# The block of the SSD's time steps as a third lane beside the first two input blocks

## The chip, the cores and the metric

The kernel runs on one core of one Trainium2 chip. The time is device microseconds (us) for one execution of the whole program. Execution times are compared as the median of runs of the same kernel.

## The reference, cut to what matters

One decoder layer over 256 positions and 2048 channels, in float32: a Mamba-2 SSD mixer, a cross-attention into 256 memory tokens, and a gated ConvFFN, each between two RMSNorms. The change lies at the very start, in the norm ahead of the SSD and in the first columns of its input projection:

```python
h = _rmsnorm(x, norm_pre[i, 0])
proj = h @ w_in                       # 2048 x (4096 + 6144 + 64)
z, xbc, dt = jnp.split(proj, ...)     # dt: the last 64 columns, one per head
xbc = silu(_causal_dwconv(xbc, conv_w, conv_b))
xs, bm, cm = jnp.split(xbc, ...)      # 4096, 8*128, 8*128
dt = softplus(dt + dt_bias)
a = dt * (-exp(a_log))
a_cs = cumsum(a, over the 128 positions of a chunk)
decay = exp(a_cs[l] - a_cs[s]) for s <= l
y_diag = (cm @ bm.T * decay) @ (xs * dt)
```

Every y of the SSD needs the decays, and so the time steps dt.

## The kernel before

**Products in three passes.** All large products are done with operands split into a high part in the fp32r type and the rest: `hi` is a copy made by ScalarE, `lo = x - hi` is made by VectorE. TensorE then adds three products, hi·hi, hi·lo and lo·hi (`mm3`, L245 to L248). The split holds for the weights (tiles `raw`, `hi`, `lo`) and for the activations (`H`, high part in columns 0 to 255, low part behind it).

**Blocks and slots.** The weights of a block of 128 output columns are one chunk of 128 x 2048 floats (1 MB): 16 steps k of 128 input channels. A chunk is loaded into one of 3 `raw` buffers on SyncE's queue and split in two halves of 1024 columns; there are 5 `hi` and 5 `lo` buffers. The work is written as a list of slots (`order`, `pos`). A slot holds one or more lanes; a lane is one block with its weights, the moving operand (`movH`), and a function `post` that takes the result out of PSUM. The lanes of a slot run step by step beside each other. Small work hangs on a slot as hooks: at a count of lane steps (`"pe"`), ahead (`early`) or behind (`late`, `tail`). The posts of a slot are written at the start of the next.

The order at the start is: slot 0 with the two lanes C0 and B0, slot 1 with the time steps' block alone (`dt`), then x0, z0, x1, z1, x2, z2, x3, z3, C1, B1 and so on, one block a slot.

**What the program order means.** The tile framework orders the instructions of each engine by a simulated timeline; what comes first in the program has the higher priority, and `hot` (`tc.high_priority`) raises it. `behind(x)` (`tc.issue_after`) keeps an instruction behind another one. On the chip each engine then runs its list in that order.

**The start.** x, transposed, comes in five pieces (`m`) between eight pieces of the two first chunks (512 columns each, `w_first` splits them). `x_h(j)` makes the high and low parts of two channel blocks, scaled by the norm's gain. The norm's factor over the channels is applied later, to the results: `x_sq(j)` squares a pair of channel blocks (ScalarE), `x_norm.add` sums them (VectorE), `pe1` sums over partitions on TensorE, GpSimd takes the power -1/2, `pe2` spreads the result over the partitions, and `rx` is its copy. Every post of the SSD's blocks begins with `x_scaled`, the product with `rx`, and so waits for it.

**The time steps' block.** Its weights are 16 steps of 64 columns (512 KB). High and low part of a step lie side by side as one operand of 128 columns, so that two matmuls a step do (`dt_mm`, L393 and L394), 32 in all; tile `hi` holds steps 0 to 7, tile `lo` steps 8 to 15. Its post leads to the chain `dt2` (softplus on VectorE and ScalarE), `dt3` (cumulative sums on TensorE), `dt4` (transpose, then a transfer to memory), `load_rows` (spread back over the partitions), `decay` (six Relu activations for each pair of heads, L505 to L507) and `decay_exp` (one Exp over four pairs, L512).

**Buffers in PSUM.** Four of the name `pj` take the blocks' results in turn, `pt` and `py` one each, `ms` two.

The names in the profile: L266 and L268 are `hilo` (in the start: the first weights), L270 and L272 are `hilo` with a scale (in the start: the parts of x), L365 the squares, L294 the sums of squares, L304 and L324 the two steps of the norm on TensorE, L332 the copy `rx`, L138 and L152 the split of the time steps' weights, L143 and L157 the splits of all later chunks, L371 `x_scaled`, L462 the Silu of the convolution.

Of the kernel before, what the change touches and what calls it, by code (L numbers as in the profile page):

```python
# [7 lines left out]
F32 = mybir.dt.float32  # L8
FR = mybir.dt.float32r
# [52 lines left out]
def hybrid_layer_kernel(ctx, tc, xT, memT, pvd, alog, w_dt, w_in, w_kv, w_q, w_out, w_o, w_up, w_dn, out):  # L62
# [64 lines left out]
        return G[:, q:q + 2].rearrange("p k n -> p (k n)")  # L127

    def split_hi(c, h):
        kind = chunks[c][2]  # L130
        if kind == "dt":
            if h == 0:
                hi = splitp.tile([128, 1024], FR, name="hi")
                lo = splitp.tile([128, 1024], FR, name="lo")
                hi_t[c, 0], lo_t[c, 0] = hi, lo
                r = raw_t[c][:, :1024].rearrange("p (k n) -> p k n", n=64)
                for t, q in ((hi, 0), (lo, 8)):
                    S.activation(t.rearrange("p (k a n) -> p k a n", a=2, n=64)[:, :, 0], r[:, q:q + 8], AF.Copy)  # L138
            return
        a, b = span(c, h)  # L140
        hi_t[c, h] = g_part(c, h, 0) if c in in_g else splitp.tile([128, 1024], FR, name="hi")
        with behind(B.get("hold_s") if c in held else None):
            S.activation(hi_t[c, h][:, :b - a], raw_t[c][:, a:b], AF.Copy)  # L143

    def split_lo(c, h):
        kind = chunks[c][2]
        if kind == "dt":
            if h == 0:
                r = raw_t[c][:, :1024].rearrange("p (k n) -> p k n", n=64)
                for t, q in ((hi_t[c, 0], 0), (lo_t[c, 0], 8)):  # L150
                    t4 = t.rearrange("p (k a n) -> p k a n", a=2, n=64)
                    V.tensor_tensor(t4[:, :, 1], r[:, q:q + 8], t4[:, :, 0].bitcast(F32), op=OP.subtract)  # L152
            return
        a, b = span(c, h)
        lo_t[c, h] = g_part(c, h, 1) if c in in_g else splitp.tile([128, 1024], FR, name="lo")
        with behind(B.get("hold_v") if c in held else None):
            V.tensor_tensor(lo_t[c, h][:, :b - a], raw_t[c][:, a:b], hi_t[c, h][:, :b - a].bitcast(F32),  # L157
                            op=OP.subtract)
# [203 lines left out]

    def x_sq(j):
        sq = wA.tile([128, 2, T], F32, name="rows" if j else "xacc", bufs=4 if j else 1)
        S.activation(sq, pair(j), AF.Square)  # L365
        x_norm.add(sq)

    def x_scaled(ps, name="ev"):
# [5 lines left out]
    def x_h(j):  # L374
        def fn():
            for k in range(2 * j, 2 * j + 2):
                now(hilo(halves(H[:, k]), m[:, k], col("pre", k)))
        return fn

    def wide(rbc):  # L380
# [7 lines left out]
    rows_d = dram.tile([NH, T], F32, name="rows_d")  # L388

    def dt_mm(c):  # L390
        def fn(ps, k):
            w = (hi_t if k < 8 else lo_t)[c, 0][:, (k % 8) * 128:(k % 8 + 1) * 128]
            PE.matmul(ps[:, :T], w, H[:, k, 0:T], start=(k == 0), stop=False)  # L393
            PE.matmul(ps[:, :T], w, H[:, k, T:], start=False, stop=(k == KD - 1))  # L394
        return fn

    def dt_post(ps):
# [225 lines left out]

    pos = {}
    for kind, i in order:
        pos[kind, i] = 0 if kind == "B" and i == 0 else slot()

    def lane(s, src, n, mov, post, wide=False):
        c = new_chunk(src, n)
# [3 lines left out]
    for kind, i in order:  # L633
        s = pos[kind, i]
        if kind in ("C", "B"):
# [1 line left out]
            lane(s, w_in[blk_no], 2048, movH, bc_post(kind + "T", blk))  # L637
            blk_no += 1
            if kind == "B":
                hook(s + 2 if i else s + 3, "pe", cb_mm(i), 2 if i else 14)  # L640
        elif kind == "dt":
            c_dt = new_chunk(w_dt, 1024, "dt")
            slots[s].lanes.append((c_dt, 0, movH, hot(dt_post), dt_mm(c_dt), False))
            hook(s + 1, "pe", hot(dt2), 2)
            hook(s + 2, "pe", hot(dt3), 4)
            hook(s + 2, "pe", hot(dt4), 11)
        elif kind == "x":
            lane(s, w_in[blk_no], 2048, movH, xs_post(i))
            blk_no += 1
            d = 2 if i < 2 else 0  # L650
            if i == 0:
                for q in range(4):
                    hook(s + 2, "early", hot(load_rows(q)))
                    hook(s + 3, "early", decay(q))
                hook(s + 3, "early", decay_exp)
            elif i % 4 == 0:
                for q in range(4):
                    hook(max(4, s - 9 + 2 * q), "early", load_rows(i + q))
                    hook(s - 7 + 2 * q, "late", decay(i + q))
                hook(s - 1, "late", decay_exp)  # L660
            if i < 2:
                hook(s + 2, "pe", xs_tr(i), 4 if i == 0 else 12)
                hook(s + 2, "late", xdt(i))
                hook(s + 3 if i == 0 else s + 2, "late", mk_m(i))
                hook(s + 4 if i == 0 else s + 3, "pe", y_mm(i), 6 if i == 0 else 10)
                hook(s + 4 if i == 0 else s + 3, "late", y_post(i))
            elif i < NP - 1:
                hook(s + 2, "early", mk_m(i))
                hook(s + 2, "pe", xs_tr(i), 4)
                hook(s + 2, "late", xdt(i))  # L670
                hook(s + 3, "pe", y_mm(i), 6)
                hook(s + 3, "late", y_post(i))
            else:
                hook(s + 1, "pe", xs_tr(i), 14)
                hook(s + 1, "late", mk_m(i))
                hook(s + 1, "late", xdt(i))
                hook(s + 2, "pe", y_mm(i), 6)
                hook(s + 2, "pe", y_post(i), 7)
        elif kind == "z":
            lane(s, w_in[blk_no], 2048, movH, z_post(i))  # L680
            blk_no += 1
        else:
            half = 0 if kind == "wo" else 1
            lane(s, w_out[half * KD + i], 2048, movG, wout_post(half, i), wide=True)
# [358 lines left out]

    for c in (0, 1, 2):
        raw_t[c] = rawp.tile([128, 2048], F32, name="raw")
    for h in range(2):
        for c in (0, 1):
            hi_t[c, h] = splitp.tile([128, 1024], FR, name="hi")  # L1050
# [2 lines left out]
    for j in range(4):  # L1053
# [1 line left out]
            nc.sync.dma_start(raw_t[c][:, 512 * j:512 * (j + 1)], chunks[c][0][:, 512 * j:512 * (j + 1)])  # L1055
        e = min(4 * j + 6, KD)
        nc.sync.dma_start(m[:, 4 * j + 2:e], xT[:, 4 * j + 2:e])
    nc.sync.dma_start(raw_t[2][:, :1024], chunks[2][0])
    nc.sync.dma_start(pv[:, PV["cw"]:], pvd[:, PV["cw"]:])
    nc.sync.dma_start(nega, bass.AP(tensor=alog.tensor, offset=alog.offset, ap=[[0, 128], [1, NH]]))  # L1060
    state.update(dma=3, hi=4, lo=4)
    make_consts()

    ps = psum.tile([128, 512], F32, name="ms", bufs=2)
# [3 lines left out]
    def w_first(j):  # L1068
        for c in (0, 1):
            q = slice(512 * (j % 2), 512 * (j % 2) + 512)  # L1070
            now(hilo((hi_t[c, j // 2][:, q], lo_t[c, j // 2][:, q]), raw_t[c][:, 512 * j:512 * (j + 1)]))

    for j in range(KD // 2):
        if j % 2 == 0:
            hook(0, "pe", lambda j=j: w_first(j // 2), 4 * j)
        hook(0, "pe", x_h(j), 4 * j)
        hook(0, "tail", lambda j=j: x_sq(j))
    hook(0, "tail", x_norm.split)
    hook(0, "tail", hot(x_norm.pe1))
# [2 lines left out]
    for i, s in enumerate(slots):  # L1082
# [1 line left out]
        need = max(ln[0] for ln in s.lanes) + 1  # L1084
        state["limit"] = 2 * min(ln[0] for ln in s.lanes) + SPLIT_BUFS
        if i == 0:
            state["limit"] = 4
        if first_up - 4 <= i < first_up:
            state["limit"] += PRE[i - first_up + 4]
        if i == first_up:  # L1090
# [15 lines left out]
        lanes = s.lanes  # L1106
        nk = max([len(ln[2]) for ln in lanes], default=0)
        cnt = 0
        names = ("pj", "pj", "pt", "py") if i == first_up else ("pj",) * 4
        pss = [psum.tile([128, 512], F32, name=n, bufs=4 if n == "pj" else 1) if ln[5] is not None else None  # L1110
               for ln, n in zip(lanes, names)]
        hooks = dict(hk.pe)
# [135 lines left out]
```

## Time and profile before

| | |
|---|---|
| median of 3 runs | 1559.93 us (1558.48 to 1560.27) |
| profiled execution | 1559.15 us |
| its span, first to last instruction | 1557.3 us |
| outside the span | 1.85 us |
| TensorE busy | 1541.5 us (99%) |
| VectorE busy | 1199.2 us (77%) |
| ScalarE busy | 963.9 us (62%) |
| granted TensorE clock, mean | 0.997 |

Matmuls are pipelined, and a matmul's busy time overlaps that of the next, so that a busy share of TensorE does not say that it ran at its peak. Times in rows are us from the start of the span, durations of single instructions are in us or ns as said. A timeline merges like instructions that follow each other: x4 and 1.71 us means four of them within 1.71 us.

### The profile page before, as it was taken

How to read it: one execution, taken by the hardware profiler on the slowest of the kernel's cores; microseconds unless marked ns; L12 is line 12 of the kernel's file. 1: busy time of each engine (PE TensorE's matmuls, PEld its weight loads, DVE VectorE, ACT ScalarE, POOL GpSimd, SP SyncE). 2: the span in 40 equal slices, each digit the busy share in tenths (PEclk: the TensorE clock that was granted, in tenths of full speed). 3: DMA queues.
4: the chain of work that ended last, by engine and by line, in shares of the span. 5: the costliest groups of instructions: out<-in, count | busy, mean ns of one | idle time of the engine just before them, and what ended most of it. 6: DMA issues, size and time to landing. Idle time of an engine off the chain costs nothing. (4 is left out here: it accounts for less than half of the span.)

```text
span 1557.3 us, 26009 instructions
## 1 busy us (share of the span) xinstructions
PE 1541.5 (99%) x10364; PEld 1418.0 (91%) x10364; DVE 1199.2 (77%) x1903; ACT 963.9 (62%) x1566; POOL 11.3 (1%) x16
## 2 busy tenths in 40 slices
PE   9999999999999999999989999999999999999998
PEld 8999999989999999889888888888888888888886
DVE  7699989755898987969788878655787866778774
ACT  7698887644777774856566655544555533555553
POOL 0000000000000000000000000000000000000000
PEclk9999999999999999999999999999999999999999
DMA  7665555655455554854444555555555555555452
GB/s 278 212 217 189 174 203 190 194 191 184 162 204 177 167 186 136 324 189 165 161 153 146 194 190 189 192 183 199 190 191 191 184 187 198 194 192 189 151 212 78
DMA packets 50937, 292.10 MB, mean 188 GB/s; under 512 B 5568, under 2 KB 9728, under 8 KB 23936
## 3 DMA queue, kind: packets, MB, share of 16 engines
q1 hardware_dynamic: 50096, 289.34, 54.3%
q8 instruction: 81, 1.33, 0.3%
q10 hardware_dynamic: 720, 1.11, 0.2%
q14 instruction: 40, 0.33, 0.1%
HBM read 288.26 MB, written 2.16 MB: 186 GB/s over the span
## 5 line engine op out<-in xcount | busy, mean ns | idle before, releaser
L143 ACT ACTIVATE hi<-raw 128x1024 fp32r<-128x1024 f32 (+2 forms) x518 | 539.9, 1045 | 480.9 <-PE pj L252 378.4
L157 DVE TENSOR_TENSOR lo<-raw,hi 128x1024 fp32r<-128x1024 f32 (+2 forms) x518 | 624.4, 1207 | 252.7 <-ACT hi L143 247.9
L252 PE MATMUL pj<-H,hi 128*128 128x512 f32 x1344 | 466.6, 392 | 1.1 <-DVE ev L931 1.1
L252 PE MATMUL pj<-G,hi 128*128 128x512 f32 x1202 | 417.1, 392 | 0.0
L246 PE MATMUL pj<-H,hi 128*128 128x256 f32 x1344 | 379.1, 283 | 1.3 <-ACT hi L266 0.8
L248 PE MATMUL pj<-H,lo 128*128 128x256 f32 x1344 | 377.9, 282 | 0.8 <-DVE lo L268 0.7
L247 PE MATMUL pj<-H,hi 128*128 128x256 f32 x1344 | 377.8, 281 | 0.0
L253 PE MATMUL pj<-H,lo 128*128 128x256 f32 x1344 | 376.2, 280 | 0.0
L253 PE MATMUL pj<-G,lo 128*128 128x256 f32 x1202 | 335.8, 280 | 0.0
L252 PEld LDWEIGHTS pj<-H,hi 128*128 128x128 f32 x1344 | 252.3, 188 | 57.0 <-ACT hi L143 1.3
L252 PEld LDWEIGHTS pj<-G,hi 128*128 128x128 f32 x1202 | 225.4, 188 | 49.5
L246 PEld LDWEIGHTS pj<-H,hi 128*128 128x128 f32 x1344 | 253.3, 189 | 3.2 <-ACT hi L266 1.6
L248 PEld LDWEIGHTS pj<-H,lo 128*128 128x128 f32 x1344 | 253.3, 189 | 2.1 <-DVE lo L268 1.7
L247 PEld LDWEIGHTS pj<-H,hi 128*128 128x128 f32 x1344 | 253.7, 189 | 1.2 <-DVE H L272 0.2
L253 PEld LDWEIGHTS pj<-H,lo 128*128 128x128 f32 x1344 | 252.5, 188 | 0.1
L253 PEld LDWEIGHTS pj<-G,lo 128*128 128x128 f32 x1202 | 225.8, 188 | 0.4
L941 DVE SCALAR_TENSOR_TENSOR fu<-ev,pv,fu 128x255 f32<-128x255 f32 (+1 forms) x176 | 84.3, 480 | 2.8
L460 DVE SCALAR_TENSOR_TENSOR u<-ev,pv,u 128x255 f32<-128x255 f32 (+2 forms) x144 | 68.7, 479 | 5.1 <-ACT u L456 3.9
L937 ACT ACTIVATE fu<-ev,pv 128x256 f32<-128x256 f32 x88 | 51.7, 589 | 1.4 <-DVE ev L934 0.9
L371 DVE TENSOR_TENSOR ev<-pj,rx 128x256 f32<-128x256 f32 x80 | 33.7, 422 | 13.4 <-PE pj L248 10.7
L266 ACT ACTIVATE Mh<-dec 128x768 fp32r<-128x768 f32 x32 | 26.9, 841 | 16.4 <-PE py L248 15.6
L934 DVE TENSOR_TENSOR ev<-ev,rb 128x256 f32<-128x256 f32 x84 | 35.5, 422 | 1.4
(287 smaller groups left out, 1461.7 us busy)
## 6 DMA issues: line engine op xcount, KB each, us to landing
raw<-in_w_up_dram SPq DMA_DIRECT2D x88, 1024.0 KB, 4.8
raw<-in_w_in_dram SPq DMA_DIRECT2D x78, 1024.0 KB, 4.9
raw<-in_w_out_dram SPq DMA_DIRECT2D x32, 1024.0 KB, 4.8
raw<-in_w_dn_dram SPq DMA_DIRECT2D x32, 960.0 KB, 4.7
raw<-in_w_dn_dram SPq DMA_DIRECT2D x16, 896.0 KB, 4.4
rows<-rows_d SPq DMA_DIRECT2D x32, 256.0 KB, 4.4
raw<-in_w_kv_dram SPq DMA_DIRECT2D x4, 1024.0 KB, 4.8
raw<-in_w_kv_dram SPq DMA_DIRECT2D x8, 512.0 KB, 4.3
```

The costliest lines, as they stand in the source:

```text
L143: S.activation(hi_t[c, h][:, :b - a], raw_t[c][:, a:b], AF.Copy)
L157: V.tensor_tensor(lo_t[c, h][:, :b - a], raw_t[c][:, a:b], hi_t[c, h][:, :b - a].bitcast(F32), op=OP.subtract)
L246: PE.matmul(ps, whi, xhi, start=start, stop=False)
L247: PE.matmul(ps, whi, xlo, start=False, stop=False)
L248: B["mm"] = PE.matmul(ps, wlo, xhi, start=False, stop=stop)
L252: PE.matmul(ps, whi, x, start=start, stop=False)
L253: B["mm"] = PE.matmul(ps[:, T:], wlo, x[:, 0:T], start=False, stop=stop)
L371: V.tensor_tensor(t, ps[:, :T], x_norm.rbc, op=OP.mult)
L460: V.scalar_tensor_tensor(u[:, d:], ps[:, :T - d], pv[:, w + j:w + j + 1], u[:, d:], op0=OP.mult, op1=OP.add)
L934: V.tensor_tensor(t, t, B["n4"].rbc, op=OP.mult)
L937: S.activation(u, t, AF.Identity, bias=col("fb", blk), scale=pv[:, w + 2:w + 3])
L941: V.scalar_tensor_tensor(u[:, d:], t[:, :T - d], pv[:, w + j:w + j + 1], u[:, d:], op0=OP.mult, op1=OP.add)
```

## The change

The time steps' block moves from slot 1 into slot 0 as a third lane, and all later slots move up by one. In the lane, a step of the time steps runs four steps behind the two others (`max(0, i - 4)`), and the last five run at the end. Its result goes to the PSUM buffer `pt` in place of a `pj`.

Its raw weights land in the tile `dec` (which the decays use later) and no longer in the third `raw` buffer. They come in two halves of 256 KB, behind the pieces 0 and 2 of x, not at the end. The load of the following chunk (x0) is issued at once, into the third `raw` buffer, ahead of the rest of the parameter vectors (`pv`) and of `nega`. The split of the time steps' weights is written between the splits of x (`dt_split`, at j = 1 and 5).

The squares of x are put behind the last high part of x on ScalarE (`behind(B["x_hi"])`).

The hooks of slot 0 move from 4j to 6j, since three lanes count three steps; the hooks `dt2`, `dt3`, `dt4` move from the counts 2, 4, 11 to 8, 8, 14 of the same blocks (x0, z0), and `cb_mm(0)` stays at z0.

```diff
     def x_sq(j):
         sq = wA.tile([128, 2, T], F32, name="rows" if j else "xacc", bufs=4 if j else 1)
-        S.activation(sq, pair(j), AF.Square)
+        with behind(B["x_hi"]):
+            S.activation(sq, pair(j), AF.Square)
         x_norm.add(sq)
...
             for k in range(2 * j, 2 * j + 2):
-                now(hilo(halves(H[:, k]), m[:, k], col("pre", k)))
+                hi, lo = halves(H[:, k])
+                B["x_hi"] = S.activation(hi, m[:, k], AF.Copy, scale=col("pre", k))
+                V.scalar_tensor_tensor(lo, m[:, k], col("pre", k), hi.bitcast(F32), op0=OP.mult, op1=OP.subtract)
...
     def dt_mm(c):
-        def fn(ps, k):
-            w = (hi_t if k < 8 else lo_t)[c, 0][:, (k % 8) * 128:(k % 8 + 1) * 128]
-            PE.matmul(ps[:, :T], w, H[:, k, 0:T], start=(k == 0), stop=False)
-            PE.matmul(ps[:, :T], w, H[:, k, T:], start=False, stop=(k == KD - 1))
+        def fn(ps, i):
+            for k in range(max(0, i - 4), i - 3 if i < KD - 1 else KD):
+                w = (hi_t if k < 8 else lo_t)[c, 0][:, (k % 8) * 128:(k % 8 + 1) * 128]
+                PE.matmul(ps[:, :T], w, H[:, k, 0:T], start=(k == 0), stop=False)
+                PE.matmul(ps[:, :T], w, H[:, k, T:], start=False, stop=(k == KD - 1))
...
-        pos[kind, i] = 0 if kind == "B" and i == 0 else slot()
+        pos[kind, i] = 0 if (kind, i) in (("B", 0), ("dt", 0)) else slot()
...
-                hook(s + 2 if i else s + 3, "pe", cb_mm(i), 2 if i else 14)
+                hook(s + 2, "pe", cb_mm(i), 2 if i else 14)
...
-            hook(s + 1, "pe", hot(dt2), 2)
-            hook(s + 2, "pe", hot(dt3), 4)
-            hook(s + 2, "pe", hot(dt4), 11)
+            hook(s + 1, "pe", hot(dt2), 8)
+            hook(s + 2, "pe", hot(dt3), 8)
+            hook(s + 2, "pe", hot(dt4), 14)
...
-    for c in (0, 1, 2):
+    for c in (0, 1):
         raw_t[c] = rawp.tile([128, 2048], F32, name="raw")
+    raw_t[2] = dec.rearrange("p a n -> p (a n)")
...
         nc.sync.dma_start(m[:, 4 * j + 2:e], xT[:, 4 * j + 2:e])
-    nc.sync.dma_start(raw_t[2][:, :1024], chunks[2][0])
+        if j in (0, 2):
+            nc.sync.dma_start(raw_t[2][:, 256 * j:256 * j + 512], chunks[2][0][:, 256 * j:256 * j + 512])
+    issue_dma(3)
     nc.sync.dma_start(pv[:, PV["cw"]:], pvd[:, PV["cw"]:])
...
-    state.update(dma=3, hi=4, lo=4)
+    state.update(dma=4, hi=6, lo=6)
...
+    def dt_split(j):
+        if j == 0:
+            hi_t[2, 0] = splitp.tile([128, 1024], FR, name="hi")
+            lo_t[2, 0] = splitp.tile([128, 1024], FR, name="lo")
+        t = (hi_t, lo_t)[j][2, 0].rearrange("p (k a n) -> p k a n", a=2, n=64)
+        now(hilo((t[:, :, 0], t[:, :, 1]), raw_t[2][:, 512 * j:512 * j + 512].rearrange("p (k n) -> p k n", n=64)))
...
         if j % 2 == 0:
-            hook(0, "pe", lambda j=j: w_first(j // 2), 4 * j)
-        hook(0, "pe", x_h(j), 4 * j)
+            hook(0, "pe", lambda j=j: w_first(j // 2), 6 * j)
+        hook(0, "pe", x_h(j), 6 * j)
+        if j in (1, 5):
+            hook(0, "pe", lambda j=j: dt_split(j // 4), 6 * j)
         hook(0, "tail", lambda j=j: x_sq(j))
...
         if i == 0:
-            state["limit"] = 4
+            state["limit"] = 6
...
-        names = ("pj", "pj", "pt", "py") if i == first_up else ("pj",) * 4
+        names = ("pj", "pj", "pt", "py") if i in (0, first_up) else ("pj",) * 4
```

Also removed are the branches of `split_hi` and `split_lo` that split the time steps' weights before.

## Rows read from the trace of the kernel before

**Rows 1.** The page, part 1: busy us, share of the span, instructions
```profile
PE 1541.5 (99%) x10364; PEld 1418.0 (91%) x10364; DVE 1199.2 (77%) x1903; ACT 963.9 (62%) x1566; POOL 11.3 (1%) x16
```

**Rows 2.** Windows: length, busy (instructions) of PE, PEld, DVE, ACT, POOL; PEclk, DMA share, GB/s
```profile
6.60:10.00 3.40, 2.91 (x18) 2.51 (x18) 1.69 (x4) 1.42 (x5) 0.00 (x0) 1.00 0.93 310
10.00:15.00 5.00, 4.12 (x30) 3.51 (x30) 4.86 (x11) 5.00 (x11) 0.00 (x0) 1.00 1.04 410
15.00:20.00 5.00, 4.64 (x34) 3.92 (x33) 5.00 (x11) 5.00 (x12) 0.00 (x0) 1.00 0.38 145
...
30.00:40.00 10.00, 10.00 (x87) 10.00 (x87) 9.22 (x16) 8.49 (x14) 0.00 (x0) 1.00 0.86 299
```

**Rows 3.** Timeline of PE, 6 to 29 us: start, us, instruction
```profile
6.66 0.56 PE L246 MATMUL pj<-H,hi 128*128 128x256 f32 x1
...
12.01 0.38 PE L246 MATMUL pj<-H,hi 128*128 128x256 f32 x1 [0.80 <-ACT hi L266]
...
23.55 0.95 PE L304 MATMUL ms<-ones,xacc 128*128 128x1 f32 x8
24.36 0.36 PE L393 MATMUL pj<-H,hi 128*128 128x256 f32 x1
24.56 0.28 PE L394 MATMUL pj<-H,hi 128*128 128x256 f32 x1
...
27.61 0.28 PE L394 MATMUL pj<-H,lo 128*128 128x256 f32 x1
...
28.42 0.28 PE L246 MATMUL pj<-H,hi 128*128 128x256 f32 x1
```

**Rows 4.** Timeline of ACT, 8 to 22 us
```profile
8.68 1.71 ACT L270 ACTIVATE H<-m,pv 128x256 fp32r<-128x256 f32 x4 [1.98 <-DMA m<-in_xT_dram]
...
10.30 1.14 ACT L365 ACTIVATE rows<-m 128x512 f32<-128x512 f32 x2
...
21.06 0.61 ACT L138 ACTIVATE hi<-raw 128x512 fp32r<-128x512 f32 x1
```

**Rows 5.** Timeline of DVE, 21 to 29 us
```profile
21.54 0.88 DVE L272 SCALAR_TENSOR_TENSOR H<-m,pv,H 128x256 fp32r<-128x256 f32 x2
22.33 0.69 DVE L294 TENSOR_TENSOR xacc<-xacc,rows 128x512 f32<-128x512 f32 x1
22.93 0.69 DVE L152 TENSOR_TENSOR hi<-raw,hi 128x512 fp32r<-128x512 f32 x1
...
28.65 0.42 DVE L332 COPY rx<-ms 128x256 f32<-128x256 f32 x1
```

**Rows 6.** Timeline of SP's queue: start, us, issue
```profile
2.59 1.07 SPq L1055 DMA_DIRECT2D raw<-in_w_in_dram  x2
3.70 0.43 SPq L1057 DMA_DIRECT2D m<-in_xT_dram  x1
```

**Rows 7.** DMA issues of 3.1:3.7 and 3.7:4.4: KB each, us to landing
```profile
raw<-in_w_in_dram SPq DMA_DIRECT2D x1, 256.0 KB, 7.1
...
m<-in_xT_dram SPq DMA_DIRECT2D x1, 512.0 KB, 7.7
```

**Rows 8.** Timeline of ACT, 36 to 39 us
```profile
37.05 1.28 ACT L462 ACT_TABLE_LOAD   x1
38.35 0.42 ACT L462 ACTIVATE xsT<-u 128x256 f32<-128x256 f32 x1
```

**Rows 9.** Timeline of ACT, 66 to 82 us
```profile
66.78 0.40 ACT L505 ACTIVATE dec<-rows,acs 128x128 f32<-128x128 f32 x1 [0.89 <-DMA rows<-rows_d]
...
73.83 2.00 ACT L143 ACTIVATE hi<-raw 128x1024 fp32r<-128x1024 f32 x2
...
78.58 2.77 ACT L512 ACTIVATE dec<-dec 128x3072 f32<-128x3072 f32 x1
```

**Rows 10.** Timeline of DVE, 74 to 77 us
```profile
74.90 2.36 DVE L157 TENSOR_TENSOR lo<-raw,hi 128x1024 fp32r<-128x1024 f32 x2 [3.89 <-ACT hi L143]
```

**Rows 11.** Timeline of PE, around 76 us
```profile
76.09 0.28 PE L246 MATMUL pj<-H,hi 128*128 128x256 f32 x1
```

More of the change, by code (lines that the diff above doesn't have):

```diff
@@ L129, in split_hi @@
     def split_hi(c, h):
[L130 to L139, printed above, removed]
         a, b = span(c, h)
@@ L145, in split_lo @@
     def split_lo(c, h):
[L146 to L153, printed above, removed]
         a, b = span(c, h)
```

## The prediction, made before the changed kernel was run

> **What bounds the kernel now.** First the busy shares: TensorE is busy for 1541.5 us of 1557.3, no other engine over 77% [rows 1]. So only what lets TensorE stand, or gives it other work, can move the end. Then the windows, to see where it stands: over the first 20 us the number of its matmuls in 5 us is 30 and 34, later 87 in 10 us [rows 2]. The start is the one stretch near the change where TensorE is short of work; there VectorE has 4.86 and 5.00 of 5 us and ScalarE 5.00 and 5.00, so the supply of split operands is the bound. From 30 us on TensorE is full, while VectorE too has 9.22 of 10.
>
> Then TensorE's timeline [rows 3]. The first product starts at 6.66, the 96 matmuls of C0 and B0 are through at 23.55, the norm's first step takes TensorE from 23.55 to 24.36, the time steps' 32 matmuls follow, and x0 begins at 28.42. In the time steps' block nothing waits: 26 steps in 3.05 us (24.56 to 27.61), 0.117 us each. What must be done ahead of x0 is then 128 x 0.117 = 15.0, plus 0.81 for the first norm step, plus 0.22 for the second (0.81 us between 27.61 and 28.42, less five matmuls): 16.0 us. It took 28.42 - 6.66 = 21.8. **The change can only win back part of these 5.7 us**; the time steps' block now runs as a solid piece behind the holes instead of in them. Last I read what feeds the holes: ScalarE's and VectorE's timelines [rows 4, 5] and the landings of the transfers [rows 6, 7].
>
> **The change part by part.**
>
> *The squares move.* One of 128x512 costs ScalarE 0.52 us (two end 1.14 after the start, the overlap taken off), its sum costs VectorE 0.60 (22.33 to 22.93) [rows 4, 5]. Six squares (the first two at 10.30) and six sums stood between the splits after 8.68; both engines were full there, so ScalarE's splits come 3.1 us earlier and VectorE's 3.6. The first square, ahead of all, goes as well, but the next pieces of x reach ScalarE at 8.68 anyway [rows 4], so I count nothing for it.
>
> *The split of the time steps' weights comes in.* Two high parts (one stood at 21.06) and two low parts, 128x512 each: 1.04 us on ScalarE, 1.2 on VectorE, taken off again.
>
> *Their transfer comes in.* 262 kB at the 310 GB/s of the windows are 0.85 us, at 410 GB/s 0.64 [rows 2]. The first half goes in behind the x that lands at 8.68, so all after it lands later: the second weight piece of B0 (issued about 3.2, landing 7.1 later, 10.3) at 11.1, the next x (3.70 + 7.7 = 11.4) at 12.2 [rows 6, 7]. The second half delays the last weights and x by as much again. No instruction of another queue is passed. SyncE then issues x0's load with no wait, so it lands some 2.5 us behind the last x (1.05 MB at 410 GB/s), near 20; `pv` and `nega` land behind it, and the posts that read them start after 29 us.
>
> *The new supply, step by step.* ScalarE: four high parts from 8.68 (0.40 each) to 10.3, the time steps' to 10.8, weights (landing 11.1) to 11.9, x from 12.2 to 13.8, weights to 14.8, x to 16.5, time steps to 17.0, weights to 18.0, the last x to 18.9. VectorE with 0.40 (two in 0.79, rows 5) and 0.60: weights' low parts end at 12.7, 15.5 and 18.9, the last x at 19.9. It was 22.4 before.
>
> *TensorE.* It has done the 24 matmuls of k = 0 to 3 by about 11, as before (the next began at 12.01, after a wait for a high part of the weights [rows 3]). From 11.4 (the first high part of the second weights) 72 + 32 are left: 104 x 0.117 = 12.2, ending at 23.6. Does the supply keep up? k = 8 comes up after 40 of them, at 16.1 (low parts 15.5); k = 12 after 72, at 19.8 (18.9); k = 14 at 21.7 (19.9). Yes, by 0.6 us at least, if the time steps' matmuls fill the gaps. For restarts I add 0.3: the step behind the norm is 0.20 in place of 0.117 (24.36 to 24.56), and I allow three or four. So 23.9.
>
> *The hand-over to x0.* The eight squares now run from 18.9 to 23.1, then x0's first high part (1.0 us each, two in 2.00 [rows 9]) ends at 24.1; its low part (about 1.15, two in 2.36 [rows 10]) follows the last sum, 23.8, and ends at 25.3, which the 16 matmuls of the first half that need high parts only cover. I take x0's start at 24.1; with both norm steps (1.0) that is 25.1 against 28.42: **3.3 us, say 3.4**, as the 0.2 of waiting can take the norm's first step in.
>
> *Bounds.* At best TensorE is never without work from 9.2 (first high part of the x landing at 8.68) on: 116 x 0.117 from there end at 22.8; with the norm 23.8: gain 4.6. At worst the last 40 matmuls (k = 12 to 15 of all three lanes and the time steps' 8 to 11) wait for the last low part, 19.9 or 0.4 later, and end at 25.0; with the norm 26.0 and one high part of x0 late by 1.0: gain 1.4.
>
> *What comes later.* `rx` was there at 29.07 [rows 5]. Its first norm step now starts near 23.9 and nothing behind it changes, so `rx` comes near 29.5, and with it all posts of C0 and B0 and the whole chain of the time steps, at about the same time as before while TensorE is 3.4 us further. The moved hooks change only the program order of that chain, and removing the lone slot takes no work away. The cover is buffers. I looked for the thinnest: the run of 24 Relus of the decays, 66.78 to 73.83 [rows 9], after which the second half of C1's weights is split at last, its low part ready near 76.05 [rows 10]. C1 starts at 76.09 (the 385th matmul of a block from x0 on) [rows 11] and needs that half 24 matmuls later, at 78.9. The margin is 2.8 us; 3.4 us of lead would turn it into a wait of 0.6. But the buffer of that half comes free earlier by the lead as well, so the split can go ahead of the Relus; I count nothing.
>
> *A rule on tables.* The change from Exp to Silu at 37.05 costs 1.28 us and the next activation starts at 38.35, right behind it [rows 8]; with the time steps' hook later, an Exp behind the first Silu would add two such changes, 2.6 us, to ScalarE and to the chain. The Trainium skill, "ScalarE: Activation LUTs", section "What ACT_TABLE_LOAD costs", puts 1.38 us of draining on top of each: 5.3 us by that. This case's trace shows no such drain at 38.35. I count neither, since ScalarE has holes there (8.49 of 10 us [rows 2]).
>
> **The sum.** The profiled execution took 1559.15 (span 1557.3 and 1.85 around it). Less 3.4: 1555.75. The median of the runs lies 0.78 above that execution: 1556.5.
>
> **The rivals.**
>
> A. *Part is given back at the decays.* The Relus stay ahead of C1's second half, and `rx` 0.5 later: a wait of 0.6 + 0.5 and the same for the next half; gain 1.3 to 2.3, 1557.6 to 1558.6. For it: the margin above. Against: the order is made anew with the lead known.
>
> B. *The lane does not fill the holes.* In program order the time steps run four k behind and five of them at the end; if TensorE's list holds to that, the holes before k = 4, 8 and 12 stay, and the two 0.75 us of transfer are lost in full: the worst bound, gain 1.4, 1558.5. Against: the order is made from what is ready, and wherever the two lanes wait, the time steps' matmuls are what is ready.
>
> C. *More.* The upper bound, 4.6, 1555.3.
>
> D. *Slower.* If Exp with its table follows the Relus directly, C1's second half is split only at 73.83 + 1.28 + 2.77 = 77.9 [rows 8, 9], its low part is ready near 80.1, and TensorE needs it at 78.9 - 3.4 = 75.5: a wait of 4.6, 1.2 more than the lead: 1559.9 + 1.2 = 1561.1. It decides from 4 us between the Relus and that split on; should the chain of the time steps also be 2 us later (the two table changes above), it costs 7 and ends at 1563.5. Against: half a chunk's split was never put behind Exp here.
>
> **How the numbers follow.** Forecast 55 in 100, A 17, B 8, C 8, D 12. The likeliest case's own range is its bounds, 1555.3 to 1558.5. For 8 in 10 I take in A, B, C and the near part of D and allow 0.4 at the low end: 1554.9 to 1560.3. A measurement of this kernel can tell 0.2% from no change, 3.1 us, so "faster" is below 1556.8: three quarters or more of the forecast (0.43) and C (0.08), 0.51. Within: the rest of the forecast, A, B and a third of D, 0.41. Slower: 0.08.
>
> **What would show it.** Right: in the changed profile no square stands on ScalarE before the last high part of x, near 18.9; L393 and L394 lie between L246 to L248 before 24; x0 begins near 24 to 25; TensorE has some 40 matmuls each in 10 to 15 and 15 to 20. `rx` at 29 to 30. No hole on TensorE between 30 and 130. Wrong: a wait of TensorE for `lo` of L157 near 24 or near 75 to 80; time steps' matmuls in one piece at the end of slot 0; more tables loaded between 30 and 60; or a changed total with the start as forecast, which would put the cause far from here.

## The result and the profile after

The changed kernel takes 1568.81 us (median; 1568.59 to 1569.81), the kernel before 1559.92 beside it: ratio 1.0061, 95% interval 1.0049 to 1.0072. It is slower by 0.6%, where 0.2% faster was forecast, and lies above the range. The profiled execution took 1568.99 us with a span of 1567.2, against 1559.15 and 1557.3: 9.8 us more to account for.

The busy shares of the page of after (against [rows 1]) show no new work:

```profile
PE 1545.2 (99%) x10364; PEld 1422.3 (91%) x10364; DVE 1199.7 (77%) x1903; ACT 966.8 (62%) x1568; POOL 12.2 (1%) x16
```

In the rows of after the lines of the kernel are others: L228 to L230 are `mm3`, L133 and L139 the splits of the chunks (high and low part of a half chunk of 1024 columns), L361 and L362 the parts of x, L348 the squares, L276 their sums, L286 and L306 the two steps of the norm on TensorE, L314 the copy `rx`, L354 `x_scaled`, L448 and L553 the Silu of the convolution and of the gates, L491 the Relus, L498 the Exp of the decays, L566 and L568 the y and its product with the gate. In the edited kernels they shift by a few.

The start, by the windows of after (columns as in [rows 2]) and TensorE's timeline, is as forecast: 44 and 44 matmuls in the two stretches that held 30 and 34, and x0 at 23.25 in place of 28.42 [rows 2, 3].

```profile
10.00:15.00 5.00, 5.00 (x44) 5.00 (x43) 4.97 (x10) 4.52 (x11) 0.00 (x0) 1.00 1.04 411
15.00:20.00 5.00, 5.00 (x44) 5.00 (x44) 4.95 (x11) 5.00 (x12) 0.00 (x0) 1.00 1.04 361
```

Compared by work, not by time, the 577th matmul of the blocks (C0 and B0 counted, the time steps' not) starts at 85.22 in after and 88.50 before: 3.3 us ahead. Of these, 1.0 is no gain: before had done six matmuls of the first y by then, which after still had ahead of it (0.118 us a step of 256 columns, 0.232 of 512). The lead of the start was 2.2 us there. The 865th starts at 135.35 against 126.94, with the same work done: TensorE is 8.4 behind. **11.7 us are lost between these two by this count, 1.0 of them for these six**, and TensorE's timeline of after says where (in brackets: idle time before, and what ended it):

```profile
23.25 0.28 PE L228 MATMUL pj<-H,hi 128*128 128x256 f32 x1
...
30.38 0.95 PE L286 MATMUL ms<-ones,xacc 128*128 128x1 f32 x8
...
99.58 0.47 PE L228 MATMUL py<-Mh,xdr 128*128 128x512 f32 x1 [1.76 <-DVE yt L566]
...
101.05 0.44 PE L524 MATMUL pt<-ident,xsT 128*128 128x128 f32 x2 [1.01 <-ACT xsT L448]
...
106.15 0.58 PE L228 MATMUL pj<-H,hi 128*128 128x256 f32 x1 [3.53 <-DVE ev L354]
106.53 0.41 PE L229 MATMUL pj<-H,hi 128*128 128x256 f32 x1
106.74 0.41 PE L230 MATMUL pj<-H,lo 128*128 128x256 f32 x1
```

Three waits, 6.3 us together; before has no hole there. The longest ends with an `ev`, the product with `rx` that empties a PSUM buffer (`x_scaled`). And behind them the steps take 0.21 us (106.53 to 106.74) in place of 0.117. The windows of after show the granted clock of that stretch:

```profile
98.00:101.00 3.00, 0.47 (x1) 0.19 (x1) 2.95 (x6) 2.97 (x5) 0.00 (x0) 1.00 0.68 178
101.00:104.00 3.00, 1.57 (x7) 1.19 (x7) 2.97 (x5) 3.00 (x9) 0.00 (x0) 0.63 0.62 248
104.00:107.00 3.00, 0.85 (x4) 0.85 (x5) 2.99 (x7) 3.00 (x10) 0.00 (x0) 0.50 0.33 83
107.00:110.00 3.00, 3.00 (x16) 3.00 (x16) 2.90 (x8) 1.61 (x5) 0.00 (x0) 0.50 0.25 87
110.00:113.00 3.00, 3.00 (x17) 2.78 (x17) 2.66 (x7) 2.30 (x4) 0.00 (x0) 0.66 0.00 0
113.00:116.00 3.00, 3.00 (x28) 3.00 (x27) 2.95 (x7) 1.93 (x5) 0.00 (x0) 1.00 0.00 0
```

TensorE had stood for most of 98 to 107; its granted clock then is 0.50, the lower level of 1.2 GHz, well into the stretch in which it is full again. From 107 to 113 it does 33 matmuls where 56 fit at the pace of 113 to 116: 23 x 3/28 = 2.5 us. The few matmuls among the waits and just behind them were slow as well. The whole: 11.7 less the three waits, a fourth of 0.2 at 128.0 and the 1.0 above leaves 4.2 for the low pace, which is also what the steps add up to when each is set against the step of its shape in before.

What made `ev` late? Follow VectorE and ScalarE of after back from there. VectorE:

```profile
18.51 0.88 DVE L362 SCALAR_TENSOR_TENSOR H<-m,pv,H 128x256 fp32r<-128x256 f32 x2
19.43 3.08 DVE L276 TENSOR_TENSOR xacc<-xacc,rows 128x512 f32<-128x512 f32 x4
22.43 2.35 DVE L139 TENSOR_TENSOR lo<-raw,hi 128x1024 fp32r<-128x1024 f32 x2
24.70 0.69 DVE L276 TENSOR_TENSOR xacc<-xacc,rows 128x512 f32<-128x512 f32 x1
25.89 0.69 DVE L276 TENSOR_TENSOR xacc<-xacc,rows 128x512 f32<-128x512 f32 x1 [0.51 <-ACT hi L133]
26.50 1.22 DVE L139 TENSOR_TENSOR lo<-raw,hi 128x1024 fp32r<-128x1024 f32 x1
27.64 0.68 DVE L276 TENSOR_TENSOR xacc<-xacc,rows 128x512 f32<-128x512 f32 x1
28.24 3.49 DVE L139 TENSOR_TENSOR lo<-raw,hi 128x1024 fp32r<-128x1024 f32 x3
31.65 0.15 DVE L291 TENSOR_SCALAR nv<-ms 128x2 f32<-128x2 f32 x1
...
35.37 0.42 DVE L314 COPY rx<-ms 128x256 f32<-128x256 f32 x1
...
98.46 0.97 DVE L566 SCALAR_TENSOR_TENSOR yt<-xsT,pv,py 64x256 f32<-64x256 f32 x2
...
101.54 0.42 DVE L568 TENSOR_TENSOR yt<-yt,sz 128x256 f32<-128x256 f32 x1
...
105.68 0.42 DVE L354 TENSOR_TENSOR ev<-pj,rx 128x256 f32<-128x256 f32 x1
```

The last low part of x ends at 19.4, as forecast (19.9). But the seven sums (the first square needs none) are no run behind it: the low parts of three half chunks stand among them, and three more ahead of `nv`. The last sum ends at 28.3, TensorE takes the norm's first step at 30.38 (23.55 before [rows 3]), and `rx` starts at 35.37 where it was 28.65 [rows 5]: 6.7 us later. ScalarE's timeline shows the same interleaving, and the rest of the chain:

```profile
18.79 2.18 ACT L348 ACTIVATE rows<-m 128x512 f32<-128x512 f32 x4
20.87 1.99 ACT L133 ACTIVATE hi<-raw 128x1024 fp32r<-128x1024 f32 x2
22.77 1.13 ACT L348 ACTIVATE rows<-m 128x512 f32<-128x512 f32 x2
...
45.44 1.28 ACT L399 ACT_TABLE_LOAD   x1
46.74 0.31 ACT L399 ACTIVATE cbm<-cbm 128x128 f32<-128x128 f32 x1
...
75.20 0.40 ACT L491 ACTIVATE dec<-rows,acs 128x128 f32<-128x128 f32 x1 [3.02 <-DMA rows<-rows_d]
...
87.45 2.77 ACT L498 ACTIVATE dec<-dec 128x3072 f32<-128x3072 f32 x1
...
104.12 0.40 ACT L553 ACTIVATE sz<-ev 128x256 f32<-128x256 f32 x1
```

The first Relu of the decays starts 8.4 us later than before, Exp 8.9 [rows 9], the first y (`yt`) at 98.46 where before it was at 88.61, 9.9 later.

Three theories were set against each other. **Theory 1**: the late `rx` makes the first y late. Until that y is multiplied by its gate, the gate buffer (`sz`, two of them) is not free, so z2's Silu can't run, its `ev` isn't free, the next results stay in PSUM, and TensorE, which is ahead, has no buffer. The trace has each link: y times `sz` at 101.54, z2's Silu at 104.12, C1's `ev` at 105.68, TensorE's step at 106.15. In the kernel before, C1's result left PSUM at 93.67, and the next `ev` at 102.01 freed a buffer for the block that starts at 108: the slack was some 5.6 us (102.43, where that `ev` ends, to 108.02). **Theory 2**: the moved hooks and the two additional table loads (45.44 and 48.51) delay the chain. **Theory 3**: the lead alone does it, TensorE running out of cover whatever the factor does.

### The profile page after: what moved, and what is told of

Same layout as the page of the kernel before. It is cut to its first block, busy times and chain, and to the rows that moved or that the text cites. A ratio compares the mean times of both kernels' runs of the same rounds, so it can differ in the third digit from the quotient of the medians.

```text
span 1567.2 us, 26032 instructions
## 1 busy us (share of the span) xinstructions
PE 1545.2 (99%) x10364; PEld 1422.3 (91%) x10364; DVE 1199.7 (77%) x1903; ACT 966.8 (62%) x1568; POOL 12.2 (1%) x16
## 5 line engine op out<-in xcount | busy, mean ns | idle before, releaser
L133 ACT ACTIVATE hi<-raw 128x1024 fp32r<-128x1024 f32 (+2 forms) x518 | 540.2, 1046 | 482.0 <-PE pj L234 377.3
L139 DVE TENSOR_TENSOR lo<-raw,hi 128x1024 fp32r<-128x1024 f32 (+2 forms) x518 | 624.5, 1208 | 264.6 <-ACT hi L133 260.2
L228 PE MATMUL pj<-H,hi 128*128 128x256 f32 x1344 | 380.4, 283 | 5.0 <-DVE ev L354 4.1
L230 PE MATMUL pj<-H,lo 128*128 128x256 f32 x1344 | 378.7, 282 | 0.1
L228 PEld LDWEIGHTS pj<-H,hi 128*128 128x128 f32 x1344 | 254.4, 189 | 6.7 <-DVE ev L354 3.8
L230 PEld LDWEIGHTS pj<-H,lo 128*128 128x128 f32 x1344 | 254.4, 189 | 0.7 <-DVE lo L139 0.3
L354 DVE TENSOR_TENSOR ev<-pj,rx 128x256 f32<-128x256 f32 x80 | 33.6, 422 | 10.4 <-PE pj L230 9.4
L248 ACT ACTIVATE Mh<-dec 128x768 fp32r<-128x768 f32 x32 | 26.9, 840 | 15.1 <-PE py L230 13.5
```

The source lines that it names most:

```text
L228: PE.matmul(ps, whi, xhi, start=start, stop=False)
L230: B["mm"] = PE.matmul(ps, wlo, xhi, start=False, stop=stop)
L354: V.tensor_tensor(t, ps[:, :T], x_norm.rbc, op=OP.mult)
```

## The experiments

**1. The squares free again** (changed kernel, not held behind the last high part):

```diff
-        with behind(B["x_hi"]):
-            S.activation(sq, pair(j), AF.Square)
+        S.activation(sq, pair(j), AF.Square)
```

> The changed kernel, with the squares of x no longer held behind the last high part. Theory 1 (the norm's factor comes late because squares and sums stand between x0's and z0's splits; posts and the time steps' chain follow it, the PSUM buffers are all held near 100 us, TensorE waits and then runs at its lower clock): the first norm step moves forward by some 6 us on TensorE, rx is there near 30 instead of 35.8, no wait over 1 us near 100, about 1557 to 1560. Theory 2 (the moved hooks of the time steps put an Exp behind the first Silu, and the chain is late by the two table changes): 1566 to 1569, the waits near 100 stay. Theory 3 (TensorE's lead alone empties the buffers, whenever the factor comes): 1564 to 1569, the waits stay.

1560.56 us, ratio to before 1.0006 (0.9997 to 1.0016): 8 us come back. The time is a little above what theory 1 allowed, and `rx` and the longest wait (1.3) miss its figures too. Its VectorE timeline and TensorE's waits from 24 to 130 us (waited for; us in total, times, longest):

```profile
32.66 0.42 DVE L314 COPY rx<-ms 128x256 f32<-128x256 f32 x1
...
94.48 0.96 DVE L565 SCALAR_TENSOR_TENSOR yt<-xsT,pv,py 64x256 f32<-64x256 f32 x2
```

```profile
PE pj L228 <- DVE ev L353: 2.0, 2, 1.3
PE pt L523 <- ACT xsT L447: 0.6, 1, 0.6
```

`rx` is still 4.0 later than before, so the hold of the squares is only part of its lateness. The same wait for `ev` is there near 100, 2.0 in place of 3.5. It shrinks with the lateness of the first y, as theory 1 says.

**2. The sums first** (changed kernel; the splits of x0, z0 and x1 held behind the last square and the last sum):

```diff
-        with behind(B.get("hold_s") if c in held else None):
+        with behind(B.get("hold_s") if c in held else B["x_sq"] if 3 <= c < 6 else None):
...
-        with behind(B.get("hold_v") if c in held else None):
+        with behind(B.get("hold_v") if c in held else B["x_sum"] if 3 <= c < 6 else None):
...
-            S.activation(sq, pair(j), AF.Square)
-        x_norm.add(sq)
+            B["x_sq"] = S.activation(sq, pair(j), AF.Square)
+        B["x_sum"] = x_norm.add(sq) or B.get("x_sum")
```

> The changed kernel, with the splits of the next three chunks (x0, z0, x1) held behind the last square on ScalarE and the last sum on VectorE, so that the norm's factor comes first. Theory 1: rx near 29 to 30, no wait near 100, the lead of the start is kept but for a short wait for x0's first split: 1555 to 1558. Theory 2: 1566 to 1569. Theory 3: 1563 to 1568, with a wait of 3 us or more near 100.

1562.24 us, 1.0016 (1.0007 to 1.0026). A miss: the sums alone don't bring `rx` back to 29. From its waits of TensorE and VectorE's timeline:

```profile
PE pj L228 <- DVE ev L354: 2.6, 2, 1.8
PE ms L286 <- DVE xacc L276: 0.8, 1, 0.8
```

```profile
33.24 0.42 DVE L314 COPY rx<-ms 128x256 f32<-128x256 f32 x1
...
96.79 0.97 DVE L566 SCALAR_TENSOR_TENSOR yt<-xsT,pv,py 64x256 f32<-64x256 f32 x2
```

The norm's first step now starts at 25.86, after a wait for VectorE, and still the factor comes at 33.2: three low parts stand ahead of `nv` (29.13) and three more behind it. This run also bears on theory 3: its lead is gone long before 100 us (the 577th matmul starts at 88.31, 0.2 ahead of before), and yet TensorE waits 2.6 us for `ev`, at 104 and 112.

**3. The hooks as before** (changed kernel):

```diff
-            hook(s + 1, "pe", hot(dt2), 8)
-            hook(s + 2, "pe", hot(dt3), 8)
-            hook(s + 2, "pe", hot(dt4), 14)
+            hook(s + 1, "pe", hot(dt2), 2)
+            hook(s + 2, "pe", hot(dt3), 4)
+            hook(s + 2, "pe", hot(dt4), 11)
```

> The changed kernel with the old counts of the time steps' hooks (2, 4, 11). Theory 1: the factor is as late as in the changed kernel, 1567 to 1570. Theory 2: the extra table changes near 45 and 48 us go, the chain is 3 us earlier, 1558 to 1563. Theory 3: 1566 to 1570.

1569.45 us, 1.0063 (1.0046 to 1.0079), with the waits of after. Its waits and ScalarE's timeline:

```profile
PE pj L228 <- DVE ev L354: 4.3, 2, 3.7
```

```profile
46.60 1.28 ACT L399 ACT_TABLE_LOAD   x1
...
49.66 1.28 ACT L448 ACT_TABLE_LOAD   x1
```

The moved hooks are not the cause; the time fits theories 1 and 3 alike. But the two additional loads, which the edit was meant to take away, are still there, so this run says nothing on what they cost. They come in run 4 as well, which has no third lane and the old hooks.

**4. The squares' move alone** (kernel before, with its two blocks and the lone slot):

```diff
-        S.activation(sq, pair(j), AF.Square)
+        with behind(B["x_hi"]):
+            S.activation(sq, pair(j), AF.Square)
...
-                now(hilo(halves(H[:, k]), m[:, k], col("pre", k)))
+                hi, lo = halves(H[:, k])
+                B["x_hi"] = S.activation(hi, m[:, k], AF.Copy, scale=col("pre", k))
...
```

> The kernel before, with one part of the change alone: the squares behind the last high part of x. Theory 1: the supply of the first two blocks is some 3 us earlier, but the factor comes some 4 to 6 us later than 29, and what the start wins is lost again near 100: 1558 to 1568, rx after 32. Theory 2: no hook is moved, so only the win of the start is left, 1557 to 1559. Theory 3: TensorE's lead is 2 to 3 us and costs as much or more: 1560 to 1564.

1561.06 us, 1.0009 (0.9999 to 1.0018). `rx` is at 32.6, but the first y at 88.40, no later than before: the later links took these 4 us in. From 24 to 130 us TensorE waits once, 1.1 us at 33.6, for a result that the late `rx` holds back; with the slower steps behind it that takes nearly all of the 2.0 us which the start had won by 30. The time is in theory 1's range, but the win of the start goes at 33 us and not near 100. So `rx` by itself doesn't tell when y comes, and with the two table loads in place (42.02, 43.64) y is not late.

**5 and 6. One more gate buffer** (changed kernel; 1 KB a partition), run twice:

```diff
-            t = wA.tile([128, T], F32, name="sz", bufs=2)
+            t = wA.tile([128, T], F32, name="sz", bufs=3)
```

> The changed kernel with a third buffer for the gates (tile sz, 2 to 3), so that one more result can leave PSUM before the first y is there; nothing else. Theory 1 (the norm's factor and with it the first y are late, and the results behind it hold all four PSUM buffers near 100 us): the order at the start stays, rx is as late as in the changed kernel (35.8), yet the waits near 100, 7 us together, shrink to under 2.5 and the lower clock behind them goes: 1557 to 1562. Rival (the late factor costs through the splits or ScalarE's order instead of the buffers): 1566 to 1570.

> The changed kernel with the third buffer for the gates once more, in more rounds. By theory 1 the lead of the start, 3.3 us by the matmuls done at 90 us, is lost in part to waits elsewhere: 1556.5 to 1559, faster than the kernel before by 0.5 to 3 us, beyond the interval.

1557.99 us, 0.9991 (0.9982 to 1.0001), and 1558.73, 0.9993 (0.9984 to 1.0002). **One buffer gives back 10.8 and 10.1 us** (10.3 and 9.8 when each is set against the kernel before that ran beside it), with the factor as late as in after. Of the first of the two: VectorE's timeline, ScalarE's, TensorE's waits from 24 to 130, and a window.

```profile
99.69 0.97 DVE L566 SCALAR_TENSOR_TENSOR yt<-xsT,pv,py 64x256 f32<-64x256 f32 x2
```

```profile
61.95 0.40 ACT L553 ACTIVATE sz<-ev 128x256 f32<-128x256 f32 x1
```

```profile
PE pj L228 <- DVE ev L354: 0.6, 1, 0.6
PE pj L230 <- DVE lo L139: 0.4, 1, 0.4
PE py L228 <- ACT Mh L248: 0.4, 1, 0.4
```

```profile
104.00:107.00 3.00, 3.00 (x28) 3.00 (x27) 2.92 (x6) 3.00 (x8) 0.00 (x0) 1.00 0.24 81
```

The first y is even later than in after (99.69), but z2's Silu no longer waits for it (61.95 in place of 104.12), and TensorE is full at a granted clock of 1.00 where it stood in after. Both came as theory 1 said in time, the first in its waits as well; but the gain is not clear of the interval, as was forecast for the second: both intervals touch 1.

**7. The same buffer in the kernel before**, as a control (same edit).

> The kernel before with the third buffer for the gates alone. Control for the run of the changed kernel with that buffer. If the buffer only takes away waits that the changed kernel has (theory 1), the kernel before, which has none near 100, stays at 1558.5 to 1560.5. If the buffer by itself is worth a microsecond or two (rival), 1556.5 to 1558.5, and then the change has won nothing.

1560.25 us, 1.0006 (0.9997 to 1.0015): there it is worth nothing, as theory 1 said.

**8. Both mendings together** (squares free, third gate buffer):

> The changed kernel with the squares free, as in the first experiment, and the third buffer for the gates. Theory 1: the waits near 100 (2.2 us) go and the lead of the start, 2.2 us, is kept: 1556 to 1558.5. Rival (what the start wins is lost for other reasons, wherever the buffers are): 1559.5 to 1561.5.

1560.36 us, 1.0005 (0.9995 to 1.0014): a miss, in the range of the rival. The only wait from 24 to 130 is 0.6 us for `xsT`, as theory 1 wants. With every matmul counted by the step of its shape, TensorE is 1.5 ahead of before at 88 us and still 1.1 at 740; then a wait of 1.3 us at 750.44, for a tile of a later stage, takes that.

**9 to 12. The factor late without the lead** (kernel before; eight powers with -1 on GpSimd put between the norm's power and its use, so that `rx` comes some 6 us later):

```diff
+            if self.name == "rx":
+                for _ in range(8):
+                    x, r = r, self.pool.tile([128, 2], F32, name="nr", bufs=2)
+                    P.tensor_tensor(r, x, mone, op=OP.pow)
...
+    mone = consts.tile([128, 2], F32, name="mone")
+    V.memset(mone, -1.0)
```

> The kernel before with eight more powers of minus one on GpSimd behind the norm's factor (an even number, so that the factor stays what it was); it delays the factor by about 4 to 6 us and gives TensorE no lead. Theory 1 with the slack that the trace of before shows (B1's result leaves PSUM at 102.4, the block that needs its buffer starts at 108.0, 5.6 us): the delay just fills the slack, waits of 0 to 2 us near 100, 1559.5 to 1563. Rival (the lead of TensorE does it, the factor's time does not matter): 1559 to 1560, no wait.

1578.2 us, 1.0119 (1.0104 to 1.0135), more than any theory said, and yet TensorE has no wait near 100. Its matmuls are slower through the whole program. That called for a look at the new constant itself: the same with a tile of 64 bytes a partition in place of 8 (`[128, 16]`), the tile alone without any power, and the powers with a tile of 1024 bytes (`[128, 256]`).

> The kernel before with eight more powers on GpSimd as before, their constant in a tile of 64 bytes a partition and not of 8, which leaves the addresses of all later tiles where they were modulo 64. If the 17 us of the first try came from those addresses: matmuls at their old pace, and by theory 1 the first y late by about 3.5 us but within the slack of 5.6, no wait near 100, 1560 to 1562.5 for the wait at the norm's second step (1.8 us). If they came from the late factor: 1575 to 1579.

> The kernel before with one more constant tile of 8 bytes a partition, written once and never read: all tiles behind it lie 8 bytes further. If addresses set the pace of the matmuls: 1574 to 1579, the matmuls of 256 columns 2 ns longer. If not: 1558.5 to 1561.

> The kernel before with the eight powers on GpSimd again, their constant now in a tile of 1024 bytes a partition. If the later tiles' addresses modulo more than 64 but at most 1024 bytes set the pace: matmuls at the pace of the kernel before, rx near 35, the first y 3 to 4 us late, by theory 1 no wait over 0.5 us near 100 since TensorE has no lead, and 1560 to 1562.5 for the wait of 1 to 2 us at the norm's second step. If the pace stays slow: 1575 to 1579.

With 64 bytes 1578.37 us, 1.0123 (1.011 to 1.0137); the 8-byte tile alone, which nothing reads, 1575.39, 1.0105 (1.009 to 1.0121); with 1024 bytes 1563.47, 1.0026 (1.0014 to 1.0038). The 64-byte run falls in the range that was given for the late factor, but the tile alone is nearly as slow, and the last run, with the same powers, is not. The pace depends on the size of this constant's tile, so only the last run can be read for the theories; at 1563.47 it is 1 us above its range. In its VectorE timeline `rx` comes 6.4 us late, as in after:

```profile
35.06 0.42 DVE L336 COPY rx<-ms 128x256 f32<-128x256 f32 x1
...
91.00 0.97 DVE L586 SCALAR_TENSOR_TENSOR yt<-xsT,pv,py 64x256 f32<-64x256 f32 x2
```

The first y is only 2.4 late there, and TensorE's one wait in 24 to 130 us is of another kind, 1.1 us at 36.09, as in run 4. By the 577th matmul TensorE is 2.7 behind before. So this run does not test what a late y does without a lead: its y is within the slack.

Lateness of the first y plus lead, by the 577th matmul, set against the slack of 5.6:

| | y late | lead | sum | waits for `ev` near 100 |
|---|---|---|---|---|
| run 12 | 2.4 | -2.7 | -0.3 | 0 |
| run 1, squares free | 5.9 | 1.8 | 7.7 | 2.0 |
| run 2, sums first | 8.2 | 0.2 | 8.4 | 2.6 |
| after | 9.9 | 3.3 | 13.2 | 3.5, and 2.8 for `yt` and `xsT` |

The second half of theory 1, from the late y through the gate buffers to TensorE's wait, stands: one buffer in that link takes the waits away (5 and 6) and is worth nothing where there are none (7). Less the slack, the sums of the last three rows are 2.1, 2.8 and 7.6. Theory 3 is not needed for the waits: run 2 waits with next to no lead, so lateness alone can do it, and a lead adds to it. What a lead does with y on time and two gate buffers was not run.

The first half of theory 1, from the late `rx` to the late y, is only a part of the cause. Starts from the traces:

| | `rx` | cumulative sums (TensorE) | first Relu | first y |
|---|---|---|---|---|
| before | 28.65 | 57.36 | 66.78 | 88.61 |
| after | 35.37 | 63.15 | 75.20 | 98.46 |
| run 1 | 32.66 | 58.59 | 70.73 | 94.48 |
| run 4 | 32.58 | 57.03 | 66.35 | 88.40 |
| run 12 | 35.06 | 59.62 | 68.84 | 91.00 |

With the two lanes (4 and 12) a factor as late as in run 1 and in after makes y late by -0.2 and 2.4, not by 5.9 and 9.9. What the rest of the change adds comes later in the chain: the cumulative sums are 1.6 later in run 1 than in run 4 and 3.5 later in after than in run 12, and the first transfer of the rows ahead of the Relus takes 5.3 and 5.5 us in place of 3.2 and 3.1. The two table loads are in all four. Which part of the change delays these links, no run takes alone.

## Why the prediction was wrong

- *The transfers, the new supply, TensorE's 128 matmuls, the hand-over to x0*: right. Last low part 19.4 (19.9 forecast), the two stretches of 44 matmuls (40), x0 at 23.25 (24.1). The size of the gain was not right for long. Counted by the work done, TensorE was 4.1 us ahead at 25, more than the 3.3 to 3.4 forecast, although the norm's first step, still to do, had gone behind x0's first 58 matmuls. By 88 us 2.2 were left; 0.6 of the loss is a wait at 36.73 for an `ev`, which stood until `rx` came. That the count of the blocks' matmuls alone gives 3.3 is luck.
- *"What comes later: its first norm step now starts near 23.9 and nothing behind it changes, so rx comes near 29.5"*: **this step failed.** It ran at 30.38 and `rx` came at 35.37. The prediction moved the squares behind the last high part and then let eight squares and their sums run as one block. On the chip ScalarE did five of them, two splits of x0's weights and then more; VectorE did six low parts among the sums and ahead of `nv`. I think the four `rows` buffers, which the squares share, and the order's simulated timeline put them so; that was argued only, no run takes this alone. The squares' hold is also not all of it: without it `rx` still comes at 32.66 (run 1). And the sentence goes on to the "whole chain of the time steps, at about the same time as before": there the rest of the change cost more than the late `rx`, the first y being 9.9 late, and 2.4 with the late `rx` alone (run 12).
- *"I looked for the thinnest [cover]: the run of 24 Relus"*: the second half of the failure. Nothing waited for C1's split at 76 to 80. The thinnest cover was PSUM, held through `ev` and `sz` by the first y; its slack, 5.6 us in the trace of before, was not worked out. Runs 5 to 7 show this link, since one buffer in it gives 10 us back to the changed kernel and none to the kernel before. The prediction's own last sign, a changed total with the start as forecast and the cause far from there, is what came.
- *The rivals.* D had the sign and the chain ("the chain of the time steps also 2 us later") but another place, the split behind Exp, and 1563.5 (its own terms, 4.6 and 2, give 1563.1). The waits found were 6.3 and not 4.6 us, and their second price, the granted clock, was in no rival: 4.2 us on top.
- *The rule on tables.* The two additional loads did come, 1.28 us each, but not through the moved hooks: they stay with the old ones (run 3). They are in runs 4 and 5 as well, where y is on time or the total is below before, so they alone cost the end nothing that these runs show. As at 38.35 before, the next activation stands right behind the load, 46.74, and the load right behind the activation ahead of it (45.02 and 0.40, then 45.44). The drain that the Trainium skill ("ScalarE: Activation LUTs", "What ACT_TABLE_LOAD costs") adds to each load is not seen here either.
- *The sum.* 11.7 lost between 85 and 135 us, less 3.3 ahead by the same count, is 8.4; some 1.5 more are lost between 740 and 760, where the granted clock of after reads 0.91 behind two short waits that both kernels have. Together 9.9 of the 9.8 found.

**What stays open.** The best version (5 and 6) ends only 1 us below before, with intervals that touch 1. In its profiles TensorE, counted by the work done, is 2.0 and 1.7 us ahead at 174 us and 1.8 and 1.4 at 740; near 745 it loses 1.5, with a granted clock of 0.91 in 740 to 760. The clock reads the same there in after and in runs 1, 3, 4, 11 and 12, but 1.00 in before and in runs 2 and 7. Whether the lead causes this, no run tests. Not all of it can be the lead's doing: run 11 is 5.6 us behind before by then, and executions of the kernel before itself differ, those with a mean granted clock of 0.998 at a median of 1559.1 us and those with 0.996 at 1560.1. At these same clocks runs 5 and 6 together stand at 1557.9 and 1558.7, 1.3 below; that is read from the spread of the runs and was not tested by itself.

## What to carry to other kernels

A lead won on the bounding engine is worth no more than the buffers between it and the slowest chain behind it: for each result that waits in PSUM, follow which later result frees its buffer, and write that slack down next to the lead and the lateness, both of which eat it. When work is moved "behind" something, look for what the order puts among it, and move the due time of everything that hangs on its last piece. If the slack falls short, look first for the one buffer in that link, which here weighed more than the order of the work. And look in the trace whether an edit took away what it was meant to: run 3 left both table loads where they were.

## What was not expected of the hardware

**A small tile changes the pace of the matmuls.** A constant of 8 bytes a partition that nothing reads made the kernel before 15.8 us slower (run 11, against the kernel before beside it); with the eight powers 8 and 64 bytes cost 18.8 each. With the powers and 1024 bytes it was 4.1, none of it pace: the matmuls take the times of the kernel before. The loss of run 11 grows through the whole program: 0.1 us at 127, 2.6 at 400, 16 at the end. From its page (busy us, mean ns of one), and under it the same line of a kernel of normal pace, the kernel before with three gate buffers:

```profile
L253 PE MATMUL pj<-H,lo 128*128 128x256 f32 x1344 | 380.2, 283 | 0.1
```

```profile
L253 PE MATMUL pj<-H,lo 128*128 128x256 f32 x1344 | 375.7, 280 | 0.0
```

It is 3 ns in these, 2 in the matmuls of 512 columns (394 and 392) and 1 to 2 in those of `mm3` in the blocks of the start (L246 to L248); with 64 bytes these here are not slower (279) and others are. The runs with 64 and 1024 bytes differ in the size of this tile alone, and I take it that the addresses of the tiles behind it do it; which tiles must lie how was not tried. An experiment that adds a small tile to such a kernel needs a control with the tile alone.

**A wait costs TensorE twice.** In after, behind the waits of 6.3 us in 8, its granted clock read 0.50 until past 110, and the steps took 0.21 us in place of 0.117: about 4.2 us more.

**GpSimd's small power takes no fixed time.** On 128x2 it took 0.70 us in the kernel before and in run 12, and 1.61 in after and in runs 1, 2 and 4, the same instruction on the critical chain of the factor (spans on GpSimd are rough in these profiles); what sets it was not tried. Its rows in the two GpSimd timelines, before and after:

```profile
24.78 0.70 POOL L315 TENSOR_TENSOR nr<-nv,mhalf 128x2 f32<-128x2 f32 x1 [23.71 <-DVE nv L309]
```

```profile
31.89 1.61 POOL L297 TENSOR_TENSOR nr<-nv,mhalf 128x2 f32<-128x2 f32 x1 [30.82 <-DVE nv L291]
```
